# Moving running sums, shifts and part of a modulation from GpSimd to VectorE, in a kernel whose instruction order is planned

## The chip, the cores and the metric

The kernel runs on one core of a Trainium2 chip. The metric is the device time of one launch in microseconds (us), as a median over runs. A core has TensorE (matrix products), VectorE, ScalarE and GpSimd (elementwise work), and SyncE, which issues the transfers. In the profile they are PE (its weight loads: PEld), DVE, ACT, POOL and SP. Each engine takes its own instructions in the order in which they are written and waits for others by semaphores.

## The reference

One step of a decoder of two layers, in float32. A layer is an FFN, a token mixing and a second FFN, each with a modulation before it and a LayerNorm after it:

```
h = x * (1 + sc1) + sh1
x = layer_norm(ALPHA * x + 0.5 * (1 + gt1) * swiglu(h, wi1, wo1))
h = x * (1 + sc2) + sh2
x = layer_norm(ALPHA * x + (1 + gt2) * mixing(h))
h = x * (1 + sc3) + sh3
x = layer_norm(ALPHA * x + 0.5 * (1 + gt3) * swiglu(h, wi2, wo2))
```

Shift, scale and gate come from conditioning vectors by a matrix of 1024 x 9216 per layer (the "ada" matrix). There are 256 tokens of one new sequence (the prompt), which share one conditioning vector, and 4 new tokens of each of 8 older ones (the samples), with a vector each. The mixing has four recurrent mixers side by side (retention, GLA, HGRN2, gated delta rule), worked in chunks; the last needs the inverse of a triangular matrix per chunk. Outputs are the activations and the updated states.

## The kernel before

Activations lie with the 1024 channels on partitions, as 8 tiles (index k or m) of 128 x 288: 256 prompt columns and 32 sample columns. For float32 accuracy each operand of a big matmul is split in a rounded part and a rest: ScalarE writes the rounded weights (`whi`), VectorE the rest (`wlo`, a subtraction over 512 columns), and a product takes three matmuls of 288 columns (`mm3`). Activations are split likewise into `hh` and `hl`. Weights stream in by transfers of 512 KB into rings of staging buffers (`st`, `stg`).

The parts that matter here:

- `modulate` (L780) makes h = x * A + B for one tile: ScalarE the prompt columns, where A and B are one number per channel; the sample columns take a multiplication and an addition of 128 x 32, on VectorE for tile 0 and on GpSimd for tiles 1 to 7. Then ScalarE rounds and VectorE subtracts. It is called in each norm that has a successor (five of them) and at the start of the program.
- `residual` (L820) adds the gated product to x for tile m, lets ScalarE square it, and GpSimd adds tile and square to a running sum `ss` of 128 x 576: for m = 1 to 6 in an FFN, for m = 1 to 4 after the mixing (`FSUM`, `WSUM`). The tiles after that go to the LayerNorm's statistics by matmuls of their own (`norm_stats`).
- `shift` (L809) subtracts the mean of the first residual tile from the others, for the accuracy of the variance. In an FFN these are 7 subtractions of 128 x 288 on GpSimd. After the mixing (`wout`, with `SUBENG` 2) they are 8, of which 5 are on GpSimd. `wout` has two parts: six of the eight mixer tiles first, the shift, then the last two tiles and the residuals.
- Other work on GpSimd stays where it is: clearing, small copies, the causal mask of the delta rule, sums of the rotary embedding, and the products of the state update (`vx`, `S0`). In the last norm four subtractions of the mean are on GpSimd.

The order of all instructions is planned on the host. The program records operations with their dependences (`Rec.add`), gives each a priority (the longest path of costs to the end, plus boosts), and `schedule` (L305) then places them one after another: it takes the engine that is free first and its ready operation of highest priority. What this fixes is the order on each engine; the chip keeps to it and takes its own time. `LB` holds boosts by the part of the program (`inv0` is the inverse of layer 0, `gates0` the eight gate projections, `glf0` the projections of GLA), for all engines or for one. `PEN` is how much priority ScalarE gives up to keep its loaded function table, `PACE` spaces filler work such as the ada matrix.

Of the kernel before, what the change touches and what calls it, by code (L numbers as in the profile page):

```python
# [19 lines left out]
DMA_LAT = 2.0  # L20
LOOK, STAY = 40, 20
SWITCH = 0.19
PEN, PACE = 5, 2
HOLD, HFRAC = {'DVE': 20, 'ACT': 20}, 0.6
LB = {'hg1': 12, 'retf0': -29, 'gdnf1': 15, 'wout1': -4, 'gla1': -3, 'hgf1': 16, 'gdnb1': 19, 'norm11': -4, 'norm01': -8, ('ret1', 'DVE'): 10, 'norm00': -20, ('norm02', 'DVE'): -20, ('ffn12', 'DVE'): -23, 'glf1': -8, 'hgf0': -15, 'ffn11': -26, ('inv0', 'ACT'): -15, 'norm02': -15, ('norm12', 'DVE'): 2, ('norm11', 'ACT'): 2, ('ret0', 'DVE'): 15, 'ffn12': 22, ('norm00', 'DVE'): 8, 'norm12': 62, ('glf0', 'PE'): 8, ('inv1', 'PE'): 8, 'ffn01': 7, 'gdnb0': -4, ('retf1', 'ACT'): 12, ('ffn02', 'DVE'): -2, ('norm00', 'PE'): 8, 'retf1': -8, ('gdnf1', 'DVE'): 4, ('ffn01', 'ACT'): -15, ('wout1', 'DVE'): -30, 'hg0': -30, ('gates1', 'DVE'): 6, ('gdnf1', 'PE'): -15, ('inv0', 'DVE'): -4, 'norm10': -53, ('gdnb0', 'DVE'): 30, 'inv0': 4, ('norm10', 'PE'): 2, 'wout0': -4, ('hgf0', 'ACT'): -30}
WIN, WARM, WARMUP = 3.413, 0.3, 20.0
KEEP, KEEP2 = 0, 0.05
DMA_RATE = 350e3
# [93 lines left out]


class Op:
    __slots__ = ("i", "eng", "fn", "args", "kw", "cost", "succ", "nd", "rt", "touch", "prio", "aset", "end", "nbytes", "start", "like", "label", "why", "prev", "act", "tiled", "boost", "side")


class Eng:
# [9 lines left out]
class Rec:  # L138
# [59 lines left out]
    def add(self, eng, attr, fn, args, kw):  # L198
        if fn == "activation" and isinstance(kw.get("bias"), (float, int)) and kw["bias"] == 0:
            kw.pop("bias")  # L200
        o = Op()
        o.i = len(self.ops)
        o.eng, o.fn, o.args, o.kw = eng, (attr, fn), args, kw
        out = args[0]
        ins = [v for v in list(args[1:]) + list(kw.values()) if isinstance(v, LV)]
        outs = [out] if isinstance(out, LV) else []
        o.cost = self.cost(eng, fn, out, ins, kw, args)
        o.act, o.tiled, o.side = 0.0, (128, 128), None
        if eng == "PE" and fn == "matmul":
            n = prod(args[2].shape[1:])  # L210
            side = lambda n: 32 if n <= 32 else 64 if n <= 64 else 128
            o.tiled = (side(args[1].p1 - args[1].p0), side(out.p1 - out.p0))
            if args[1].dtype != F32R and o.tiled != (128, 128):
                o.side = kw.get("tile_position") or (0, 0), 2 * ((out.p1 - out.p0) / 1200 + 0.006), 4 * n / 2400 + 0.003
            area = (args[1].p1 - args[1].p0) * (out.p1 - out.p0) / 16384
            o.act = area * (n / 2400 if args[1].dtype == F32R else n / 600)
        o.nbytes = 0
        if fn == "dma_start":
            v = out if isinstance(out, LV) else args[1]
            o.nbytes = 4 * prod(v.shape)  # L220
            if eng == "POOL":
                o.cost = 0.15
        rw = fn == "copy_predicated" or (fn == "matmul" and kw.get("start") is False)
        o.aset = ACT_SET.get(args[2]) if fn == "activation" else None
        deps, touch = set(), {}
        for v in ins + (outs if rw else []):
            r = v.region()
            touch[id(v.t)] = v.t
            for (j, w, q) in v.t.acc:
                if w and j != o.i and overlap(q, r):  # L230
                    deps.add(j)
            v.t.acc.append((o.i, False, r))
        for v in outs:
            r = v.region()
            touch[id(v.t)] = v.t
            keep = []
            for (j, w, q) in v.t.acc:
                if j != o.i and overlap(q, r):
                    deps.add(j)
                    if covers(r, q):  # L240
                        continue
                elif j == o.i and covers(r, q):
                    continue
                keep.append((j, w, q))
            keep.append((o.i, True, r))
            v.t.acc[:] = keep
        if fn == "matmul":

            start, single = kw.get("start", True), kw.get("start", True) and kw.get("stop", True)
            q0, q1 = out.p0 // 32, (out.p1 + 31) // 32  # L250
            for (j, a, b, one) in out.t.mms:
                if j != o.i and a < q1 and q0 < b and (not (single and one) if start else one is not None):
                    deps.add(j)
            out.t.mms.append((o.i, q0, q1, single if start else None))
        o.touch = list(touch.values())
        for t in o.touch:
            t.left += 1
        o.succ, o.nd, o.rt, o.prio, o.like, o.label, o.why = [], 0, 0.0, 0.0, self.fill, self.label, ('start', -1)
        o.nd, o.boost = len(deps), self.boost + LB.get(self.label, 0.0) + LB.get((self.label, eng), 0.0)
        for j in deps:  # L260
            self.ops[j].succ.append(o.i)
        self.ops.append(o)
        return o
# [41 lines left out]
    def schedule(self):  # L305
# [15 lines left out]
        busy = dict.fromkeys(engs, 0.0)  # L321
        dense, run, tiled = False, 0, (128, 128)
        tiles = {}
        win, wact, warm = 0, 0.0, False
        recent, racts = collections.deque(), 0.0

# [32 lines left out]
        while len(order) < len(ops):  # L359
            best = None  # L360
            for e in engs:
                if avail[e]:
                    t = free[e]
# [64 lines left out]
            if e == "PE":  # L428
                a = o.act
                if o.tiled != tiled:  # L430
                    tiled, run = o.tiled, 0
                    c += SWITCH
                    tiles = {}
                f = 1 if warm else 2
                if o.side:

                    (r0, c0), ld, st = o.side
                    w = max([x for (r1, c1), x in tiles.items() if (r1 == r0 or tiled[0] == 128) and (c1 == c0 or tiled[1] == 128)], default=0.0)
                    extra = max(0.0, w - t)
                    late = t + (c - o.cost) + extra + f * max(ld, st)  # L440
                    tiles[r0, c0] = late
                    c += extra - o.cost + ld
                run += 1
                recent.append((t, a))
                racts += a
                if not warm:
                    c += 0.0 if o.side else o.cost
                b = (win + 1) * WIN
                if t + c > b:
                    wact += a * (b - t) / c  # L450
                    n = int((t + c) / WIN)
                    warm = wact / WIN > WARM or n > win + 1 and a > WARM * c
                    win, wact = n, a * (t + c - n * WIN) / c
                else:
                    wact += a
            if o.aset is not None and o.aset != cur:
                cur = o.aset
                c += 1.28
# [164 lines left out]
class Net:  # L623
# [156 lines left out]
    def modulate(self, k, xs, A, B, hh, hl, h=None, cuts=((0, NT),)):  # L780

        nc = self.nc
        if h is None:
            h = self.tmp()
        for c0, c1 in cuts:
            c1 = min(c1, TP)
            if MODACT:
                nc.scalar.activation(h[:, c0:c1], xs[:, c0:c1], AF.Identity, bias=B[:, k, 0:1], scale=A[:, k, 0:1])
            else:
                nc.vector.tensor_scalar(h[:, c0:c1], xs[:, c0:c1], A[:, k, 0:1], B[:, k, 0:1], op0=ALU.mult, op1=ALU.add)  # L790
        hs = h[:, TP:].rearrange("p (b t) -> p b t", t=TS)
        eng = nc.gpsimd if k else nc.vector
        eng.tensor_tensor(hs, xs[:, TP:].rearrange("p (b t) -> p b t", t=TS), bc(A[:, k, 1:9], 2, TS), op=ALU.mult)
        eng.tensor_tensor(hs, hs, bc(B[:, k, 1:9], 2, TS), op=ALU.add)
        for c0, c1 in cuts:
            o = nc.scalar.activation(hh[:, k, c0:c1], h[:, c0:c1], AF.Copy)
        nc.vector.tensor_sub(hl[:, k, :], h, hh[:, k, :])
        return o
# [10 lines left out]
    def shift(self, x0, first, tag, nv=0):  # L809
# [4 lines left out]
        self.mm(psc, self.ones128, x0)  # L814
        nc.scalar.activation(c, psc, AF.Copy)
        for j in range(first, KD):
            (nc.vector if j <= nv else nc.gpsimd).tensor_tensor(xa[:, j, :], xa[:, j, :], c, op=ALU.subtract)
        return c

    def residual(self, m, ps, G, nsum, slast=1, shifted=False):  # L820
# [18 lines left out]

            nc.scalar.activation(self.t([P, 1], "pre"), d[:, m, 1, 0:1], AF.Exp, scale=-1.0)  # L840
        if m == 1:
            nc.gpsimd.tensor_tensor(ss, d[:, 0, :, :], d[:, 1, :, :], op=ALU.add)
        elif 1 < m < nsum:
            nc.gpsimd.tensor_tensor(ss, ss, d[:, m, :, :], op=ALU.add)
        nc.boost = 0.0
        self.nsum, self.slast = nsum, slast

# [1242 lines left out]
```

## Time and profile before

| | |
|---|---|
| runs | 1537.78 us median of 3 (1537.45 to 1544.69) |
| profiled execution | 1532.65 us, span on the core 1530.8 us |
| mean granted TensorE clock | 0.967 of full speed |
| busy | TensorE 1446.6, VectorE 909.5, ScalarE 712.5, GpSimd 226.0 us |
| HBM | 263.52 MB read, 176 GB/s over the span |

The busy time of an engine counts instructions from start to end; back to back they overlap by a little, as the next begins before the last one has left the pipeline. A matmul of 288 columns is shown with about 0.3 us, while one starts every 0.133 us at full clock. Nearly all lines are L539, the one that emits each planned operation, so groups are told apart by their tiles. "Chain" is the work that ended last, followed back from the end: at each step to what released it.

### The profile page before, as it was taken

What the parts mean: (1) busy time and instruction counts of PE and PEld (TensorE: products, weight loads), DVE (VectorE), ACT (ScalarE), POOL (GpSimd) and SP (SyncE); (2) the same over time, 40 slices, a digit from 0 to 9 for tenths busy, and PEclk for the clock granted to TensorE, in tenths of its full rate; (3) what the DMA queues carried; (4) which work ended last, traced back from release to release, by engine and by line L of the source; (5) the groups of instructions that cost most, each with busy time, mean ns of one, the idle gap of its engine ahead of it and who ended that gap; (6) DMA issues with size and microseconds to landing.
All of it is one profiled execution on the core that took longest, in us unless ns stands there. A gap on an engine that the chain in (4) does not pass through costs nothing.

```text
span 1530.8 us, 32584 instructions
## 1 busy us (share of the span) xinstructions
PE 1446.6 (94%) x13172; PEld 1353.6 (88%) x13172; DVE 909.5 (59%) x1922; ACT 712.5 (47%) x1449; POOL 226.0 (15%) x347
## 2 busy tenths in 40 slices
PE   7899998989998989999999999988999997999996
PEld 6899998888986869999999999977888885999996
DVE  3555555867366895555565555477269578555564
ACT  4544434853312465444474444476132644644443
POOL 0000023210013340002120003132000325000031
PEclk9999999999999999999999999998599999999998
DMA  9856576655445655555555556455032364555530
GB/s 359 327 179 209 177 264 202 232 184 180 159 171 189 214 207 181 166 165 168 168 213 183 165 166 208 150 176 184 27 97 65 112 218 176 194 166 165 166 123 31
DMA packets 80215, 271.11 MB, mean 177 GB/s; under 512 B 9376, under 2 KB 12992, under 8 KB 80064
## 3 DMA queue, kind: packets, MB, share of 16 engines
q1 hardware_dynamic: 80064, 269.03, 52.6%
q8 instruction: 103, 1.69, 0.4%
q14 instruction: 48, 0.39, 0.1%
HBM read 263.52 MB, written 5.47 MB: 176 GB/s over the span
## 4 chain that ended last, share of the span: by engine, by line
PE 81%; DVE 9%; ACT 5%; issue 2%; DMA 2%; SPq 0%; POOL 0%; DVEq 0%; ACTq 0%; POOLq 0%
PE psum_acc L539 48%; PE psum_ps L539 25%; PE psum_ada L539 3%; DVE base_d L539 3%; PE psum_phB L539 2%; PE psum_phA L539 2%; DVE base_wlo L539 1%; ACT base_whi L539 1%; ACT base_tmp L539 1%; ACT L538 1%; PE psum_oa L539 1%; DVE base_tmp L539 1%; DMA gp_stg<-wi 1%; DMA base_st<-win 1%; DVE mx_qxA L539 1%
## 5 line engine op out<-in xcount | busy, mean ns | idle before, releaser
L539 ACT ACTIVATE base_whi<-base_st 128x512 fp32r<-128x512 f32 x410 | 252.1, 624 | 271.1 <-PE psum_acc L539 205.2
L539 DVE TENSOR_TENSOR base_wlo<-base_st,base_whi 128x512 fp32r<-128x512 f32 x410 | 294.1, 725 | 135.4 <-ACT base_whi L539 123.8
L539 DVE TENSOR_TENSOR gp_wlog<-gp_stg,gp_whig 128x512 fp32r<-128x512 f32 x274 | 198.1, 727 | 279.6 <-ACT gp_whig L539 278.5
L539 ACT ACTIVATE gp_whig<-gp_stg 128x512 fp32r<-128x512 f32 x274 | 171.4, 628 | 297.7 <-PE psum_acc L539 261.5
L539 PE MATMUL psum_ps<-base_hh,base_whi 128*128 128x288 f32 x760 | 192.0, 299 | 4.1 <-ACT base_hh L539 4.1
L539 PE MATMUL psum_ps<-base_hl,base_whi 128*128 128x288 f32 x760 | 186.2, 297 | 0.8 <-DVE base_hl L539 0.8
L539 PE MATMUL psum_ps<-base_hh,base_wlo 128*128 128x288 f32 x760 | 185.7, 296 | 0.0
L539 PE MATMUL psum_acc<-base_hh,gp_whig 128*128 128x288 f32 x648 | 168.1, 304 | 8.0 <-ACT base_hh L539 5.0
L539 PE MATMUL psum_acc<-base_hh,base_whi 128*128 128x288 f32 x552 | 162.0, 326 | 13.9 <-ACT base_hh L539 7.1
L539 PE MATMUL psum_acc<-base_hl,gp_whig 128*128 128x288 f32 x648 | 162.5, 296 | 0.0
L539 PE MATMUL psum_acc<-base_hh,gp_wlog 128*128 128x288 f32 x648 | 157.2, 296 | 0.0
L539 PE MATMUL psum_acc<-base_hl,base_whi 128*128 128x288 f32 x552 | 155.8, 312 | 0.4
L539 PE MATMUL psum_acc<-base_hh,base_wlo 128*128 128x288 f32 x552 | 155.0, 312 | 0.4 <-DVE base_wlo L539 0.4
L539 PEld LDWEIGHTS psum_ps<-base_hh,base_whi 128*128 128x128 f32 x760 | 132.5, 190 | 6.2 <-ACT base_hh L539 4.6
L539 PEld LDWEIGHTS psum_ps<-base_hl,base_whi 128*128 128x128 f32 x760 | 130.2, 189 | 1.7 <-DVE base_hl L539 1.5
L539 PEld LDWEIGHTS psum_ps<-base_hh,base_wlo 128*128 128x128 f32 x760 | 130.2, 189 | 0.2
L539 PEld LDWEIGHTS psum_acc<-base_hh,base_whi 128*128 128x128 f32 x552 | 104.5, 200 | 26.2 <-ACT base_hh L539 7.8
L539 PEld LDWEIGHTS psum_acc<-base_hh,gp_whig 128*128 128x128 f32 x648 | 112.6, 189 | 13.0 <-ACT base_hh L539 6.9
L539 PE MATMUL psum_acc<-gp_gl,gp_whig 128*128 128x288 f32 x384 | 113.9, 297 | 0.0
L539 PE MATMUL psum_acc<-gp_gh,gp_whig 128*128 128x288 f32 x384 | 113.8, 296 | 0.0
L539 PE MATMUL psum_acc<-gp_gh,gp_wlog 128*128 128x288 f32 x384 | 113.2, 295 | 0.0
L539 PEld LDWEIGHTS psum_acc<-base_hl,gp_whig 128*128 128x128 f32 x648 | 112.4, 189 | 0.3 <-DVE base_hl L539 0.2
(429 smaller groups left out, 2773.4 us busy)
## 6 DMA issues: line engine op xcount, KB each, us to landing
base_ast<-ada_w SPq DMA_DIRECT2D x135, 512.0 KB, 6.5
gp_stg<-wi SPq DMA_DIRECT2D x82, 512.0 KB, 3.6
base_st<-wi SPq DMA_DIRECT2D x82, 512.0 KB, 3.6
base_st<-win SPq DMA_DIRECT2D x60, 512.0 KB, 3.6
gp_stg<-wo SPq DMA_DIRECT2D x48, 512.0 KB, 3.5
base_st<-wo SPq DMA_DIRECT2D x40, 512.0 KB, 3.5
base_st<-wout SPq DMA_DIRECT2D x16, 512.0 KB, 4.6
gp_stg<-wi SPq DMA_DIRECT2D x14, 256.0 KB, 6.8
```

What stands on the lines that cost most here:

```text
L538: nc.scalar.preload_act_table_set(cur)
L539: getattr(getattr(nc, o.fn[0]), o.fn[1])(*[conv(a) for a in o.args], **{k: conv(v) for k, v in o.kw.items()})
```

## The change

Sums, shifts and the samples' modulation are issued on VectorE for all tiles. The planner gets a rule: an operation `tensor_tensor` or `tensor_sub` on VectorE or GpSimd without an operand in PSUM is marked `port`; if the other engine has such a one running at the time it is placed, its cost grows by what is left of that. Two constants and 32 boosts change.

```diff
-PEN, PACE = 5, 2
+PEN, PACE = 8, 1.5
...
-LB = {
...
-'gla1': -3, 'hgf1': 16, 'wout0': -4, 'inv0': 4, ('inv0', 'ACT'): -15, ('glf0', 'PE'): 8, 'norm10': -53, 'norm12': 62
+'gla1': 5, 'hgf1': 8, 'wout0': 15, 'inv0': -11, ('inv0', 'ACT'): -45, 'glf0': 30, 'norm10': -31, 'norm12': 88
+('glf0', 'ACT'): 30, 'gates0': -8, ('gates0', 'DVE'): 2, 'gates1': 4, 'ret1': 4
...
+        o.port = eng in ("DVE", "POOL") and fn in ("tensor_tensor", "tensor_sub") and not any(v.t.tag.pool == "psum" for v in ins)
...
+        port = {"DVE": (0.0, 0.0), "POOL": (0.0, 0.0)}
...
+            if o.port:
+                a, b = port["POOL" if e == "DVE" else "DVE"]
+                if a <= t < b:
+                    c += b - t
+                port[e] = t, t + c
...
-        eng = nc.gpsimd if k else nc.vector
-        eng.tensor_tensor(hs, xs[:, TP:].rearrange("p (b t) -> p b t", t=TS), bc(A[:, k, 1:9], 2, TS), op=ALU.mult)
-        eng.tensor_tensor(hs, hs, bc(B[:, k, 1:9], 2, TS), op=ALU.add)
+        nc.vector.tensor_tensor(hs, xs[:, TP:].rearrange("p (b t) -> p b t", t=TS), bc(A[:, k, 1:9], 2, TS), op=ALU.mult)
+        nc.vector.tensor_tensor(hs, hs, bc(B[:, k, 1:9], 2, TS), op=ALU.add)
...
-            (nc.vector if j <= nv else nc.gpsimd).tensor_tensor(xa[:, j, :], xa[:, j, :], c, op=ALU.subtract)
+            nc.vector.tensor_tensor(xa[:, j, :], xa[:, j, :], c, op=ALU.subtract)
...
-            nc.gpsimd.tensor_tensor(ss, d[:, 0, :, :], d[:, 1, :, :], op=ALU.add)
+            nc.vector.tensor_tensor(ss, d[:, 0, :, :], d[:, 1, :, :], op=ALU.add)
...
-            nc.gpsimd.tensor_tensor(ss, ss, d[:, m, :, :], op=ALU.add)
+            nc.vector.tensor_tensor(ss, ss, d[:, m, :, :], op=ALU.add)
```

The boost of `inv1` (8 on TensorE) stays.

## Rows read from the trace of the kernel before

**Rows 1.** The page: busy us of each engine, share of the span, instructions.
```profile
PE 1446.6 (94%) x13172; PEld 1353.6 (88%) x13172; DVE 909.5 (59%) x1922; ACT 712.5 (47%) x1449; POOL 226.0 (15%) x347
```

**Rows 2.** The page's chain of waits: share of the span by engine.
```profile
PE 81%; DVE 9%; ACT 5%; issue 2%; DMA 2%; SPq 0%; POOL 0%; DVEq 0%; ACTq 0%; POOLq 0%
```

**Rows 3.** Table of stretches: busy us per engine, granted clock, DMA share, GB/s.
```profile
core 0: us, PE busy (x) PEld busy (x) DVE busy (x) ACT busy (x) POOL busy (x), PEclk, DMA share, GB/s
380.00:450.00 70.00, 68.96 (x1125) 63.50 (x1123) 34.50 (x68) 16.17 (x36) 3.19 (x4) 1.00 0.47 156
518.00:556.00 38.00, 36.10 (x330) 29.55 (x328) 31.43 (x78) 15.95 (x35) 12.44 (x12) 1.00 0.38 126
716.00:776.00 60.00, 60.00 (x452) 60.00 (x451) 33.94 (x57) 27.85 (x47) 16.08 (x13) 1.00 0.51 156
...
1060.00:1120.00 60.00, 57.64 (x740) 52.43 (x740) 23.56 (x53) 18.50 (x39) 0.61 (x1) 0.72 0.19 63
1262.00:1290.00 28.00, 23.20 (x193) 15.44 (x192) 23.79 (x53) 10.39 (x26) 17.22 (x18) 0.94 0.28 96
```

**Rows 4.** VectorE's timeline, layer 0's output projection: start, duration, operation.
```profile
544.48 0.18 DVE L539 TENSOR_TENSOR base_d<-base_rt,base_xa 128x32 f32<-128x32 f32 x1
544.58 0.87 DVE L539 SCALAR_TENSOR_TENSOR base_d<-psum_ps,base_G,base_xa 128x256 f32<-128x256 f32 x2
545.37 1.93 DVE L539 TENSOR_TENSOR base_wlo<-base_st,base_whi 128x512 fp32r<-128x512 f32 x1
...
552.61 0.94 DVE L539 TENSOR_TENSOR base_d<-base_rt,base_xa 128x32 f32<-128x32 f32 x1
```

**Rows 5.** GpSimd's timeline in the same stretch.
```profile
545.34 1.41 POOL L539 TENSOR_TENSOR base_d<-base_d 128x576 f32<-128x576 f32 x1 [3.61 <-issue]
```

**Rows 6.** The chain in order of time: start, length, what.
```profile
309.65 2.38 DVE base_tmp L539
...
1225.55 1.37 DVE base_wlo L539
...
1278.54 1.40 DVE base_d L539
...
1283.36 1.90 DVE base_wlo L539
```

**Rows 7.** GpSimd's groups: count, busy us, mean ns, idle before and its releaser.
```profile
L539 POOL TENSOR_TENSOR base_d<-base_d 128x576 f32<-128x576 f32 x32 | 45.6, 1425 | 162.5 <-ACT base_d L539 158.8 <-issue 3.6
L539 POOL TENSOR_TENSOR base_xa<-base_xa,base_tmp 128x288 f32<-128x288 f32 x38 | 37.9, 1023 | 475.9 <-ACT base_tmp L539 457.2 <-DVE base_xa L539 14.8 <-issue 3.7
...
L539 POOL TENSOR_TENSOR base_d<-base_d,base_hA 128x32 f32<-128x32 f32 x35 | 12.9, 368 | 39.2 <-DVE base_d L539 31.9 <-DVE base_tmp L539 7.2
...
L539 POOL TENSOR_TENSOR base_tmp<-base_tmp,base_hB 128x32 f32<-128x32 f32 x7 | 2.1, 314 | 0.1
```

**Rows 8.** VectorE's timeline where GpSimd is idle: pairs of equal instructions.
```profile
562.14 0.81 DVE L539 TENSOR_TENSOR base_d<-base_d 128x288 f32<-128x288 f32 x2
...
577.55 1.29 DVE L539 TENSOR_TENSOR base_wlo<-base_st,base_whi 128x512 fp32r<-128x512 f32 x2
```

**Rows 9.** VectorE's timeline in layer 0's first norm.
```profile
269.54 0.49 DVE L539 TENSOR_TENSOR base_d<-base_d 128x288 f32<-128x288 f32 x1
...
270.69 0.50 DVE L539 TENSOR_TENSOR base_d<-base_d 128x288 f32<-128x288 f32 x1
```

**Rows 10.** Timelines of VectorE and GpSimd in the conv of layer 0.
```profile
298.87 0.54 DVE L539 SCALAR_TENSOR_TENSOR base_tmp<-base_tmp,base_cvec,base_tmp 128x312 f32<-128x312 f32 x1
...
298.87 0.60 POOL L539 COPY mx_gcso<-base_tmp 128x3 f32<-128x3 f32 x2 [0.82 <-ACT base_tmp L539]
```

**Rows 11.** ScalarE's groups: the loads of function tables.
```profile
L538 ACT ACT_TABLE_LOAD x30 | 38.5, 1283 | 1.2 <-PEq L2077 0.7
```

**Rows 12.** The chain in the two inverses.
```profile
401.58 1.99 PE psum_ps L539 x64
...
1083.60 3.56 PE psum_ps L539 x64
1087.16 1.02 PE psum_acc L539 x3
```

More of the change, by code (lines that the diff above doesn't have):

```diff
@@ L22 @@
 SWITCH = 0.19
-PEN, PACE = 5, 2
+PEN, PACE = 8, 1.5
 HOLD, HFRAC = {'DVE': 20, 'ACT': 20}, 0.6
-LB = {'hg1': 12, 'retf0': -29, 'gdnf1': 15, 'wout1': -4, 'gla1': -3, 'hgf1': 16, 'gdnb1': 19, 'norm11': -4, 'norm01': -8, ('ret1', 'DVE'): 10, 'norm00': -20, ('norm02', 'DVE'): -20, ('ffn12', 'DVE'): -23, 'glf1': -8, 'hgf0': -15, 'ffn11': -26, ('inv0', 'ACT'): -15, 'norm02': -15, ('norm12', 'DVE'): 2, ('norm11', 'ACT'): 2, ('ret0', 'DVE'): 15, 'ffn12': 22, ('norm00', 'DVE'): 8, 'norm12': 62, ('glf0', 'PE'): 8, ('inv1', 'PE'): 8, 'ffn01': 7, 'gdnb0': -4, ('retf1', 'ACT'): 12, ('ffn02', 'DVE'): -2, ('norm00', 'PE'): 8, 'retf1': -8, ('gdnf1', 'DVE'): 4, ('ffn01', 'ACT'): -15, ('wout1', 'DVE'): -30, 'hg0': -30, ('gates1', 'DVE'): 6, ('gdnf1', 'PE'): -15, ('inv0', 'DVE'): -4, 'norm10': -53, ('gdnb0', 'DVE'): 30, 'inv0': 4, ('norm10', 'PE'): 2, 'wout0': -4, ('hgf0', 'ACT'): -30}
+LB = {'hg1': 12, 'retf0': -29, 'gdnf1': 15, 'glf0': 30, 'wout1': -6, 'gla1': 5, 'hgf1': 8, 'gdnb1': 19, 'norm11': -2, ('ret1', 'DVE'): 10, 'norm00': -20, ('norm02', 'DVE'): -20, ('ffn12', 'DVE'): -23, 'ret1': 4, 'glf1': -10, 'hgf0': -15, 'ffn11': -26, ('inv0', 'ACT'): -45, 'norm02': -15, ('norm12', 'DVE'): 2, ('norm11', 'ACT'): 2, ('ret0', 'DVE'): 15, 'ffn12': 22, ('norm00', 'DVE'): 6, 'norm12': 88, ('inv1', 'PE'): 8, 'ffn01': 7, 'gdnb0': -6, ('retf1', 'ACT'): 12, ('ffn02', 'DVE'): -2, ('norm00', 'PE'): 12, 'retf1': -8, ('gdnf1', 'DVE'): 4, ('ffn01', 'ACT'): -15, ('wout1', 'DVE'): -30, 'hg0': -30, ('gates1', 'DVE'): 6, ('gdnf1', 'PE'): -15, ('inv0', 'DVE'): -4, 'norm10': -31, ('gdnb0', 'DVE'): 30, 'inv0': -11, ('norm10', 'PE'): 2, 'wout0': 15, ('hgf0', 'ACT'): -30, ('gla0', 'PE'): 2, ('hgf1', 'PE'): -4, 'gdnf0': -2, ('gates1', 'ACT'): -15, ('norm12', 'ACT'): 30, ('gla1', 'ACT'): -15, ('retf0', 'ACT'): 8, 'gates0': -8, ('glf0', 'ACT'): 30, ('norm02', 'ACT'): -4, ('norm00', 'ACT'): -4, ('gates0', 'DVE'): 2, ('wout1', 'ACT'): -30, ('gdnf1', 'ACT'): -2, 'gates1': 4}
 WIN, WARM, WARMUP = 3.413, 0.3, 20.0
@@ L124 @@
 class Op:
-    __slots__ = ("i", "eng", "fn", "args", "kw", "cost", "succ", "nd", "rt", "touch", "prio", "aset", "end", "nbytes", "start", "like", "label", "why", "prev", "act", "tiled", "boost", "side")
+    __slots__ = ("i", "eng", "fn", "args", "kw", "cost", "succ", "nd", "rt", "touch", "prio", "aset", "end", "nbytes", "start", "like", "label", "why", "prev", "act", "tiled", "boost", "side", "port")
 class Eng:
```

## The prediction, made before the change was run

> **What bounds the kernel now.** I read the engine shares first: TensorE is busy for 94% of the span, VectorE 59%, GpSimd 15% [rows 1]. The chain of waits puts 81% of the span on TensorE, 9% on VectorE, 5% on ScalarE and 0% on GpSimd [rows 2]. These averages hide two kinds of stage, so I read a table of stretches next [rows 3]. In the second matmul of an FFN (716 to 776 us) TensorE is busy 60.00 of 60 us, VectorE 33.94, GpSimd 16.08: whatever VectorE or GpSimd do there is covered. Around the mixers' output projection (518 to 556 and 1262 to 1290 us) VectorE is busy 31.43 of 38 and 23.79 of 28 us, and in the second TensorE only 23.20 of 28: there VectorE sets the pace. The triangular inverse of layer 0 lies in 380 to 450 us at a granted clock of 1.00 (2.4 GHz); that of layer 1 in 1060 to 1120 us at a mean of 0.72, so more than half of that stretch is at 1.2 GHz.
>
> Last I read VectorE instruction by instruction beside GpSimd. In layer 0's output projection an addition of two 32-column tiles takes 0.18 us at 544.48, but 0.94 at 552.61, and a 512-column subtraction takes 1.93 us at 545.37 [rows 4]. The long subtraction lies beside a GpSimd running sum, 1.41 us from 545.34 [rows 5], and its excess is about as long as that sum. There are four such instructions in that stretch. Layer 1 has them on the chain itself: 1.40 us at 1278.54 for a 32-column addition, 1.90 us at 1283.36 for a 512-column subtraction [rows 6]. So two elementwise instructions on SBUF tiles, one on each engine, run in turn.
>
> **The change part by part.**
>
> *What leaves GpSimd.* 32 running sums (45.6 us), 38 shift subtractions (37.9 us) and 42 pairs of modulation, which are four groups from 12.9 to 2.1 us, 29.6 together [rows 7]: 113 of its 226 us. What comes to VectorE is counted from one start to the next. 32-column instructions are 0.18 us long and start 0.10 apart (544.48 and 544.58 [rows 4]), so ends overlap by 0.08. Two of 512 columns end to end take 1.29 us and two of 288 take 0.81 [rows 8]: alone 0.69 and 0.45, apart 0.60 and 0.37. By that slope 576 columns cost 0.67 (an estimate). Sum: 32 x 0.67 + 38 x 0.37 + 84 x 0.10 = 44 us more VectorE work, less the time for which it was held by the work that moves.
>
> *In the FFNs* (6 sums and 7 shifts each): 6 x 0.67 + 7 x 0.37 = 6.6 us, beside a TensorE that is full while VectorE has 26 of 60 us free [rows 3]. Cost 0. Queued behind a sum are the splits of later weights; these run ahead of their matmuls by several tiles, so they can slip by a sum. If the last one can't, 0.67 us per FFN: 2.7 us, kept for the range.
>
> *In the two output projections* (4 sums and 5 shifts each). VectorE gets 4 x 0.67 + 5 x 0.37 = 4.5 us more. In layer 0 it loses what the sums held it: four instructions, the first by 1.93 - 0.69, the last by 0.94 - 0.18, together 3.8 us. So VectorE taken alone ends up 0.7 us later: one end. The other end takes both engines as one resource, as they run in turn: a sum shrinks from 1.42 to 0.67 us, a shift from 1.02 (the mean [rows 7]) to 0.37; 4 x 0.75 + 5 x 0.65 = 6.3 us earlier. Layer 1's stretch is nearer the second end (GpSimd busy 17.22 of 28 us), layer 0's nearer the first (12.44 of 38) [rows 3]. I take the middle, 2.5 us in each: -5. The state updates queued on GpSimd behind the shifts come earlier; nothing on the chain waits for them.
>
> *In the norms* (7 pairs each). Before the mixers VectorE works without a pause through three 288-column operations per tile, 1.15 us from 269.54 to 270.69 [rows 9]. A pair adds 0.20 us if other work lies between its halves, 0.39 if not (two of 0.18, and a gap). It removes some 0.05 us of hold (0.49 and 0.50 there, 0.45 undisturbed). So 7 x 0.15 = 1 us each in the two norms before mixers: +2. Before an FFN the twelve matmuls of a tile (12 x 0.133, from 452 in 60 us) take 1.6 us, longer than VectorE's turn, and the first tile was on VectorE already: 0. At the start of the program the pairs lie behind transfers: 0. Ends: +13.7 (5 norms x 7 x 0.39) and -2 (5 x 7 x 0.05, where only the hold goes).
>
> *The planner's new rule.* 17 instructions on the chain are held by work that stays on GpSimd (state updates, the causal mask, rotary sums), together 12.6 us over their undisturbed lengths. The first is the product of 2.38 us at 309.65 (288 columns, 0.45 undisturbed), the last the subtraction of 1.37 us at 1225.55 [rows 6]. The planner now sees such a wait when it places what follows, but it places by priority and looks for no way round it. Ends 0 and -12.6; I take a third: -4.
>
> In the conv a three-operand instruction on SBUF tiles takes 0.54 us beside two GpSimd copies, which take 0.60 [rows 10]; held for them it would end no earlier than 1.1 us after its start. The Trainium skill (SBUF — State Buffer, section "SBUF: two separate sides") says that any VectorE instruction with two SBUF inputs and any GpSimd instruction that reads SBUF shut each other out. The trace agrees for the additions above and does not for this copy. By the page the planner's rule, which knows two-operand arithmetic only, would misplace the 36 conv instructions, and less of the 4 us would be won; by the row it misses nothing there.
>
> *PEN 5 to 8.* ScalarE loads a table 30 times, 38.5 us [rows 11], 1.28 each. A higher penalty may save loads; one saved on the chain gives 1.28. Ends 0 and -13 (ten of them); I take two: -2.5.
>
> *PACE and the boosts* reorder everything within a stage. The trace shows what an order can be worth: a group of 64 small inverse matmuls takes 1.99 us in layer 0 and 3.56 in layer 1, and the big ones between layer 1's groups 1.02 for three, 0.34 each [rows 12] against 0.133. Layer 1 has four groups of 64 and four of 32 in this state, and some 24 big ones: 4 x 1.57 + 4 x 0.79 + 24 x 0.2 = 14 us. So layer 1 could win up to 14 us and layer 0 lose as much. I take 0, and keep both ends.
>
> Sum: -5 + 0 + 2 - 4 - 2.5 + 0 = -9.5 us. The profiled execution took 1532.65 us (1530.8 of span and 1.85 around it), 5.1 less than the median of the timed runs, 1537.78; so it would go to 1523.2 and the median to 1528.3. I say **1528 us**, with its own range from 1519 to 1535.
>
> **The rivals.** Half a per cent, 7.7 us, is about what a measurement of this kernel can tell from no change.
> - *A better order too* (1514 us). The new priorities also put projections among layer 1's inverse, its clock stays at 2.4 GHz, and the 14 us come on top. For it: that stretch moves 63 GB/s only [rows 3], so weights could be brought there. Against it: inv1's own boosts stay as they are.
> - *Layer 0's inverse loses its cover* (1549 us, slower). The diff puts inv0 from 4 to -11, its ScalarE work from -15 to -45, and glf0 up to 30, so the projections that now lie between its groups can be spent before it. Then layer 0 pays the 14 us; the output projections and norms still give 3, planner and tables nothing: 1537.8 - 3 + 14. It decides from a mean granted clock under about 0.8 in that stretch. Against it: gates0, eight projections, goes down to -8 and is left to fill.
> - *Nothing comes of it* (1539 us). VectorE takes on as much as it was held (0.7 us late at one output projection, even at the other), the norms cost 2 and a saved load pays for it; the planner places as before. For it: GpSimd is 0% of the chain [rows 2].
>
> **How the numbers follow.** Forecast 0.45, better order 0.15, lost cover 0.2, nothing 0.2. Faster by over 0.5% (under 1530.1): 0.15 and four fifths of 0.45, so 0.51. Slower by over 0.5% (above 1545.5): 0.2 and some of the dear end of the norms, 0.22. Between them 0.27. The range takes in most of the first rival and the second up to its price: 1511 to 1549.
>
> **What would show it.** GpSimd busy near 113 us, VectorE between 915 and 935. In the residuals no 32-column addition over 0.3 us. The second part of each output projection up to the norm some 2.5 us shorter. Tiles before the mixers every 1.3 us instead of 1.15. Fewer than 30 table loads. The clock over both inverses, which tells the first two rivals apart. The prediction is wrong if the sums push weight splits so far that TensorE waits in the FFNs, or if the order moves a whole stage by more than 10 us.

## The result, and the profile after

The kernel after takes 1526.4 us (median of 6 runs, 1518.8 to 1533.59); the kernel before, run beside it, 1543.64 (6 runs, 1537.45 to 1545.15). The ratio is 0.9898, with an interval of 0.9863 to 0.9933. Later, on another chip, it was 1522.38 and 0.9879 (0.9850 to 0.9907). So it is faster by 1.0 to 1.2%, and 1528 was near. It was near for the wrong reasons, as the experiments show.

The engine shares of the kernel after answer to [rows 1], its chain to [rows 2]:

```profile
PE 1450.7 (95%) x13172; PEld 1355.8 (89%) x13172; DVE 922.0 (60%) x2076; ACT 710.4 (47%) x1447; POOL 112.9 (7%) x193
```
```profile
PE 81%; DVE 9%; DMA 4%; ACT 4%; issue 1%; SPq 0%; ACTq 0%; DVEq 0%; POOL 0%
```

GpSimd lost exactly the 113 us that were moved, VectorE has 922, and the chain is as it was. Nothing here tells where the 17 us came from, so I cut the span into stages: each ends with the last matmul of a LayerNorm's statistics. They are FFN, mixing of layer 0, FFN; FFN, mixing of layer 1, FFN; the rest is the last norm. The profile of before that I had was an unusually quick execution (1532.65 us at a clock of 0.967; 62 timed runs with a clock on record have a median of 1542.6 at 0.959), so a second profile of before stands here (1540.51 us, 0.959), then the kernel after (1528.0 us). The columns are those of [rows 3]:

```profile
core 0: us, PE busy (x) PEld busy (x) DVE busy (x) ACT busy (x) POOL busy (x), PEclk, DMA share, GB/s
0.00:261.22 261.22, 246.47 (x2313) 236.95 (x2313) 130.72 (x272) 116.82 (x227) 28.88 (x49) 0.99 0.71 243
261.22:564.91 303.69, 281.25 (x3119) 243.24 (x3123) 202.16 (x461) 127.07 (x271) 61.97 (x97) 0.91 0.53 182
564.91:787.50 222.59, 218.47 (x1625) 215.81 (x1629) 127.65 (x245) 114.54 (x228) 24.59 (x34) 0.98 0.57 179
787.50:1011.60 224.10, 222.11 (x1855) 219.54 (x1858) 123.02 (x240) 109.50 (x219) 25.09 (x36) 1.00 0.55 179
1011.60:1297.89 286.29, 264.87 (x2570) 226.72 (x2573) 195.87 (x448) 129.73 (x274) 61.47 (x101) 0.92 0.38 126
1297.89:1526.15 228.26, 221.68 (x1708) 218.30 (x1708) 121.57 (x236) 109.19 (x220) 21.12 (x28) 0.99 0.47 152
```
```profile
0.00:254.41 254.41, 242.16 (x2252) 232.91 (x2256) 132.98 (x295) 119.00 (x229) 5.62 (x17) 1.00 0.71 249
254.41:563.84 309.43, 289.62 (x3194) 249.16 (x3194) 199.78 (x488) 125.07 (x270) 49.57 (x79) 0.90 0.53 182
563.84:785.29 221.45, 216.78 (x1603) 215.08 (x1607) 131.67 (x271) 115.25 (x228) 3.63 (x7) 0.98 0.54 176
785.29:1010.32 225.03, 222.68 (x1862) 219.57 (x1866) 126.11 (x267) 109.56 (x219) 3.99 (x10) 1.00 0.56 180
1010.32:1292.11 281.79, 263.12 (x2674) 224.89 (x2674) 197.24 (x472) 127.91 (x275) 46.61 (x77) 0.95 0.42 143
1292.11:1513.88 221.77, 216.39 (x1600) 214.19 (x1599) 125.40 (x262) 108.33 (x218) 0.25 (x1) 0.99 0.44 138
```

The differences are -6.8, +5.7, -1.1, +0.9, -4.5 and -6.5, with -0.2 in the last norm -12.5 us. So these profiles have the gain in the first and the last FFN, and the two mixings nearly cancel. Look at TensorE's instruction counts: the first FFN has 61 matmuls fewer, the last 108 fewer, and the mixings have them: by their tiles 60 and 104 of these are small matmuls of the ada matrix, which the planner uses as filler. Look then at the clock in the mixings: lower in layer 0, higher in layer 1. The stretches of [rows 3] show it closer up, in the kernel after:

```profile
380.00:450.00 70.00, 66.36 (x865) 60.71 (x864) 28.90 (x63) 13.21 (x29) 0.61 (x1) 0.74 0.47 163
1060.00:1120.00 60.00, 57.29 (x560) 53.36 (x558) 40.53 (x91) 29.69 (x60) 4.27 (x14) 0.96 0.42 135
```

In the first profile of before these were 1.00 and 0.72, in the second 0.83 and 0.71. The chain says it by groups of 64 small matmuls of the inverse, as in [rows 12] (start, length, what); the first row is layer 0's, the second layer 1's:

```profile
423.56 3.56 PE psum_ps L547 x64
...
1147.25 1.99 PE psum_ps L547 x64
```

Four of layer 0's five groups of 64 now take what four of layer 1's took, and layer 1's take what layer 0's took. But part of this was there before: in one order, the same group of layer 0 ran at either rate (first profile of before, then the second):

```profile
416.59 1.99 PE psum_ps L539 x64
...
415.91 3.56 PE psum_ps L539 x64
```

The clock did what the two rivals on the order said, one in each layer. The price did not follow: against the second profile layer 0's mixing pays 5.7 us and layer 1's gets 4.5, of 14 each. Against the first, from which the prediction was made, it is 16.0 and 7.1. In TensorE's order layer 1's inverse has 369 matmuls of 288 columns between its first and last group, 50 before. Layer 0's has as many as before (285 for 288), but none between its last eight groups, where 96 stood.

### The profile page after: what moved, and what is told of

It reads as the page before. It is cut to its first block, busy times and chain, and to the rows that moved or that the text cites. A ratio compares the mean times of both kernels' runs of the same rounds, so it can differ in the third digit from the quotient of the medians.

```text
span 1526.2 us, 32521 instructions
## 1 busy us (share of the span) xinstructions
PE 1450.7 (95%) x13172; PEld 1355.8 (89%) x13172; DVE 922.0 (60%) x2076; ACT 710.4 (47%) x1447; POOL 112.9 (7%) x193
## 4 chain that ended last, share of the span: by engine, by line
PE 81%; DVE 9%; DMA 4%; ACT 4%; issue 1%; SPq 0%; ACTq 0%; DVEq 0%; POOL 0%
PE psum_acc L547 47%; PE psum_ps L547 24%; DVE base_d L547 3%; PE psum_ada L547 3%; PE psum_phA L547 3%; PE psum_phB L547 3%; DMA base_st<-win 2%; PE psum_oa L547 1%; ACT base_tmp L547 1%; DMA base_ast<-ada_w 1%; DVE base_wlo L547 1%; ACT base_whi L547 1%; DVE base_hl L547 1%; DVE base_tmp L547 1%; DVE base_xa L547 1%
## 5 line engine op out<-in xcount | busy, mean ns | idle before, releaser
L547 DVE TENSOR_TENSOR base_wlo<-base_st,base_whi 128x512 fp32r<-128x512 f32 x410 | 282.9, 698 | 143.4 <-ACT base_whi L547 133.2
L547 DVE TENSOR_TENSOR gp_wlog<-gp_stg,gp_whig 128x512 fp32r<-128x512 f32 x274 | 188.0, 690 | 262.3 <-ACT gp_whig L547 241.9
L547 PE MATMUL psum_ps<-base_hh,base_whi 128*128 128x288 f32 x760 | 197.6, 301 | 8.2 <-ACT base_hh L547 7.9
L547 PE MATMUL psum_ps<-base_hl,base_whi 128*128 128x288 f32 x760 | 191.1, 298 | 0.0
L547 PE MATMUL psum_ps<-base_hh,base_wlo 128*128 128x288 f32 x760 | 189.8, 298 | 0.5 <-DVE base_wlo L547 0.5
L547 PEld LDWEIGHTS psum_ps<-base_hl,base_whi 128*128 128x128 f32 x760 | 133.3, 191 | 0.5 <-DVE base_hl L547 0.4
```

The costliest lines, as they stand in the source:

```text
L547: getattr(getattr(nc, o.fn[0]), o.fn[1])(*[conv(a) for a in o.args], **{k: conv(v) for k, v in o.kw.items()})
```

## The experiments

First the direct work. The planner was left as in the kernel before, and so was the order; in the traces TensorE's and ScalarE's instructions stand in the same order one for one, and only the engine that executes the moved operations changes (`Eng` takes the engine to plan for and the one to issue on):

```diff
+        self.moved = Eng(self, "POOL", "vector")
...
-        eng = nc.gpsimd if k else nc.vector
+        eng = nc.moved if k else nc.vector
...
-            nc.gpsimd.tensor_tensor(ss, ss, d[:, m, :, :], op=ALU.add)
+            nc.moved.tensor_tensor(ss, ss, d[:, m, :, :], op=ALU.add)
```

> The kernel before with its planned order kept to the last instruction: the sums, shifts and samples' modulation are planned as GpSimd work with GpSimd's costs, and only issued on VectorE. It measures the move by itself. My theory (the move gives a little, the order the rest): 2 to 6 us faster than before, GpSimd busy 113 us, no 32-column addition in a residual over 0.3 us. 'All of it is the order': within 2 us of before. 'All of it is the end of the mutual holds': 12 to 18 us faster, as the changed kernel.

Measured 1546.0 us, ratio 1.0009 (0.9998 to 1.0019): the move by itself gains nothing. The holds did go. VectorE in layer 0's output projection, to be held against [rows 4]; the third row is a running sum:

```profile
553.22 0.18 DVE L540 TENSOR_TENSOR base_d<-base_rt,base_xa 128x32 f32<-128x32 f32 x1
553.32 0.87 DVE L540 SCALAR_TENSOR_TENSOR base_d<-psum_ps,base_G,base_xa 128x256 f32<-128x256 f32 x2
554.11 0.75 DVE L540 TENSOR_TENSOR base_d<-base_d 128x576 f32<-128x576 f32 x1
554.77 0.69 DVE L540 TENSOR_TENSOR base_wlo<-base_st,base_whi 128x512 fp32r<-128x512 f32 x1
...
560.36 0.18 DVE L540 TENSOR_TENSOR base_d<-base_rt,base_xa 128x32 f32<-128x32 f32 x1
```

Of 48 such 32-column additions none takes over 0.2 us; before, nine took over 0.3, the longest 1.40. But a sum costs VectorE 0.66 us from start to start. From the first residual addition to the end of the stage it is 10.73 us in layer 0 (second profile of before: 11.89) and 13.91 in layer 1 (14.47): 1.2 and 0.6 us gained (the shifts lie before this stretch). The norms before mixers lose what was forecast: a tile takes 1.30 us instead of the 1.15 of [rows 9] (the two halves of a tile's pair now stand among its three operations),

```profile
268.63 0.45 DVE L540 TENSOR_TENSOR base_hl<-base_d,base_hh 128x288 fp32r<-128x288 f32 x1
...
269.94 0.45 DVE L540 TENSOR_TENSOR base_hl<-base_d,base_hh 128x288 fp32r<-128x288 f32 x1
```

and the last tile's split comes 0.6 and 1.4 us later after the norm's statistics. The two middle FFNs are 0.8 and 0.9 us longer (223.35 and 224.98), the first is the same; the last is 1.4 us shorter, with 3.4 us less at 1.2 GHz.

The counterpart is the kernel after, planned as it is, with the moved operations executed on GpSimd again:

```diff
+        self.moved = Eng(self, "DVE", "gpsimd")
...
-        nc.vector.tensor_tensor(hs, hs, bc(B[:, k, 1:9], 2, TS), op=ALU.add)
+        eng = nc.moved if k else nc.vector
+        eng.tensor_tensor(hs, hs, bc(B[:, k, 1:9], 2, TS), op=ALU.add)
```

> The changed kernel with its planned order kept, and the moved work issued on GpSimd again. It undoes the move by itself. My theory: 8 to 14 us faster than before, so 3 to 8 us slower than the changed kernel. 'All of it is the order': 13 to 18 us faster than before, like the changed kernel. 'All of it is the end of the holds': within 3 us of before.

Measured 1527.38 us, ratio 0.9882 (0.9855 to 0.9909): the whole gain is there without the move. (The profiled execution, 1515.54 us at a clock of 0.977, was the quickest of the six.) GpSimd's groups show its work back, and eight of the 32-column additions take over 0.3 us again, up to 1.32:

```profile
L548 POOL TENSOR_TENSOR base_d<-base_d 128x576 f32<-128x576 f32 x32 | 47.4, 1482 | 159.8 <-ACT base_d L548 146.4 <-issue 13.0
L548 POOL TENSOR_TENSOR base_xa<-base_xa,base_tmp 128x288 f32<-128x288 f32 x38 | 36.3, 987 | 151.9 <-ACT base_tmp L548 150.7 <-DVE base_xa L548 1.2
```

The stretch from the first residual addition to the end of the stage, which the prediction wanted 2.5 us shorter, is 10.1 and 10.7 us in the kernel after (1.8 and 3.8 less than before), and 9.8 and 10.0 here, without the move. So it is the order. Which part of the change makes it? The kernel after with all constants of before, boosts included, and the kernel after without the rule:

```diff
-PEN, PACE = 8, 1.5
+PEN, PACE = 5, 2
...
-LB = {
+LB = {
...
```

> The changed kernel with PEN, PACE and all boosts of before: the move and the planner's rule, without the new constants. My theory (the constants carry most of the order's gain): between 8 us faster and 10 us slower than before, and slower than the changed kernel by 8 us or more. 'The rule and the move do it, the constants are detail': 12 to 18 us faster than before.

Measured 1542.65 us, ratio 0.9993 (0.9980 to 1.0006), inside my range. Its profile has 704 ada matmuls in the first FFN, as before, and 64 of the 104 in the last; these two take 262.7 and 227.3 us.

```diff
-            if o.port:
+            if False:
```

> The changed kernel with the planner's rule off (no operation pays for the other engine): the move and the new constants. If the rule is what matters in the planning: 5 us or more slower than the changed kernel, and more than 5 us of held VectorE time on the chain again. If the move and the constants do it: within 4 us of the changed kernel. I expect 3 to 10 us slower than the changed kernel.

Measured 1541.74 us, ratio 0.9990 (0.9972 to 1.0009): 15 us slower than the changed kernel, more than I expected. In its profile layer 0's mixing takes 318.9 us, with 75.1 us at 1.2 GHz, and the last FFN 227.6, with 64 ada matmuls; the kernel after has 309.4, 64.9, 221.8 and none. I read the two results as "only all three together give the good order". The next kernel, the one before with the new constants and nothing else, refuted that:

```diff
-PEN, PACE = 5, 2
+PEN, PACE = 8, 1.5
...
-LB = {
...
+'gla1': 5, 'hgf1': 8, 'wout0': 15, 'inv0': -11, ('inv0', 'ACT'): -45, 'glf0': 30, 'norm10': -31, 'norm12': 88
...
```

> The kernel before with the new PEN, PACE and LB alone: nothing is moved to VectorE and the planner doesn't know the rule. Its planned order has two features of the kernel after that the kernel before lacks: some 500 matmuls of gates and norms stand between the groups of layer 1's inverse (before: 136), and some 50 of the modulation's matmul pairs have left the last feed-forward. Theory A (the gain is those features of the order, wherever they come from): 1524 to 1533 us, the profile shows layer 1's inverse at about 29 ns per matmul and the last feed-forward near 222 us. Theory B (the constants were fitted to one planner and give a good order only with the rule and the move): 1540 to 1547 us, as the two kernels with half of the change measured. Theory C (the move is needed at run time after all, because the new order brings GpSimd's work against VectorE's): the order's features are there but the stretches with running sums, shifts and modulation are longer, 1535 to 1540 us.

Measured 1515.32 us (1502.73 to 1520.51), ratio 0.9819 (0.9786 to 0.9852): theory A, and more than it expected. This beats the kernel after, with GpSimd as busy as ever (227.2 us). Its first, layer 1's and last stage:

```profile
0.00:255.63 255.63, 243.06 (x2252) 233.95 (x2256) 129.41 (x268) 118.81 (x229) 26.39 (x44) 1.00 0.71 247
...
1006.75:1278.17 271.42, 254.25 (x2655) 216.21 (x2658) 194.59 (x448) 127.48 (x272) 63.11 (x100) 0.97 0.44 144
1278.17:1500.51 222.34, 217.60 (x1623) 214.63 (x1623) 121.76 (x236) 109.02 (x221) 21.64 (x28) 0.99 0.46 143
```

The first and the last stage are nearly as in the kernel after, and layer 1's mixing is 10 us shorter still, at a clock of 0.97. Does the move help in this better order? The same order with the moved operations issued on VectorE (the edit of the first experiment, with the new constants):

```diff
+        self.moved = Eng(self, "POOL", "vector")
...
-PEN, PACE = 5, 2
+PEN, PACE = 8, 1.5
```

> The kernel before with the new PEN, PACE and LB, and the running sums, shift and samples' modulation issued on VectorE; they are planned as GpSimd's, so that the order is exactly that of the kernel with the constants alone (1515.3 us), which leaves them on GpSimd. Theory A (what GpSimd holds on VectorE costs nothing in any of these orders): 1512 to 1519 us, the same. Theory B (the move is worth its 5 us where the order doesn't waste it): 1507 to 1511 us. Theory C (VectorE's extra work is late in the mixings, where it is busiest): 1519 to 1526 us.

Measured 1516.78 us, ratio 0.9852 (0.9811 to 0.9893). This overlaps the one above, so no gain is seen again; a loss of some us can't be told from none, as six runs of this order spread over 13 us.

Another order for layer 1's mixing, found by changing nine boosts of the kernel after:

```diff
+('glf1', 'ACT'): 2, ('gla0', 'ACT'): -11, ('ret1', 'PE'): -15, ('norm11', 'ACT'): -6, 'gdnb1': 15, 'hg1': 16
...
```

> The kernel after with nine boosts changed, eight of them labels of the mixings; first feed-forward, layer 0's mixing and the two middle feed-forwards are planned as in the kernel after, layer 1's mixing gets another order. Theory A (the order decides, and each covered stretch of TensorE is worth its microseconds): stages up to layer 1's mixing within 1 us of the kernel after at the same granted clock, layer 1's mixing 3 to 8 us shorter, 1518 to 1524 us. Theory B (orders of this quality differ by chance, about 15 us between any two): anywhere from 1520 to 1545 us, and the earlier stages move too. Theory C (the granted clock evens it out): 1526 us, the gained time comes back as stretches at half clock.

Measured 1524.83 us, ratio 0.9897 (0.9871 to 0.9923). The earlier stages repeat within 0.5 us and layer 1's mixing is 5.2 us shorter in the profile (276.6), both as theory A said. The median, though, is that of the kernel after (1522.38 beside it) and just outside theory A's range; theory C can't be told from A by this.

Second profiles of both kernels:

> The kernel after unchanged, a second profile. Theory A (times of one order follow where TensorE falls to half clock): 1518 to 1534 us; the four feed-forward stages repeat within 0.5 us, the two mixings differ between the two executions by 0.2 to 0.5 us for each us more at half clock. Theory B (the scatter comes from the DMAs): the feed-forwards differ too, by a us or more, at the same half-clock time.

> The kernel before unchanged, a second profile, since the first was of an execution of 1532.65 us, under all its timed runs. Theory A (its scatter is the half clock in layer 0's mixing): 1539 to 1548 us, layer 0's mixing near 302 us with over 40 us at half clock, all other stages within 1.5 us of the first profile. Theory B (the first profile's execution was quick in all stages): every stage 0.5 to 2 us longer.

Before: 1540.51 us, mixing of layer 0 303.7 us instead of 293.4, with 54.6 us at 1.2 GHz instead of 27.3 in the same order; other stages within 2.6 us, where theory A allowed 1.5. After: 1522.38 us in the median, the profiled execution 1531.37; its other FFNs and both mixings repeat within 0.2 us, but the first FFN is 2.9 us longer (with 3.4 us at 1.2 GHz for none), which theory A didn't allow. One order is thus not one time: some stretches fall to half clock in one execution and not in the next.

Last, the two features of the new order (matmuls among layer 1's inverse, ada matmuls out of the last FFN) one at a time in the kernel before, each by one number, and `PACE`:

```diff
+'inv1': -4
```

> The kernel before with one number changed: layer 1's inverse has a boost of -4. Everything up to layer 1's mixing is planned as before; there, 429 matmuls of gates and projections stand between the groups of the inverse, before 136; ten of the modulation's pairs more than before leave the last feed-forward. Theory A (layer 1's inverse at half clock is what the mixing loses): its groups go from 53 to about 29 ns per matmul, layer 1's mixing is 6 to 11 us shorter, 1532 to 1537 us. Theory B (the cover costs what it gives, since the matmuls between the groups delay the inverse and the projections wait for it): 1540 to 1545 us though the clock is up. Theory C (the half clock moves elsewhere): 1540 to 1545 us, with the same microseconds at half clock in another place.

Measured 1535.96 us, ratio 0.9975 (0.9951 to 0.9999), in theory A's range for the time. In its profile the inverse's first groups still run at half clock before the later ones take 1.99 us per 64; but the mixing takes 285.98 us, as before, which is what theory B says of it. The median clock of its runs is 0.9645 against 0.959. Where its gain lies is thus not shown.

```diff
+('inv1', 'DVE'): 8
```

> The kernel before with one number changed: VectorE's work of layer 1's inverse has a boost of 8. Everything up to layer 1's mixing is planned as before and the inverse has the same 137 matmuls between its groups; 62 of the modulation's pairs (124 matmuls) have gone from the last feed-forward into layer 1's mixing. Theory A (they fill gaps in the mixing, while the feed-forward has none): the last feed-forward goes from 227 to 222 us, the mixing is 0 to 2 us longer, 1538 to 1541 us. Theory B (TensorE's work is only moved): the mixing is 4 to 5 us longer, 1542 to 1545 us.

Measured 1545.01 us, ratio 1.0026 (1.0001 to 1.0052): theory B, and worse. Layer 1's mixing and the last FFN:

```profile
1011.66:1310.79 299.13, 278.22 (x2676) 237.38 (x2675) 196.46 (x449) 129.42 (x274) 62.49 (x101) 0.90 0.38 126
1310.79:1533.76 222.97, 217.01 (x1600) 214.01 (x1598) 121.51 (x234) 109.16 (x221) 22.87 (x28) 0.99 0.47 149
```

The FFN gains 5.3 us, as expected; the mixing pays 12.8, as its clock falls to 0.90.

```diff
-PEN, PACE = 5, 2
+PEN, PACE = 5, 1.5
```

> The kernel before with PACE 1.5 for 2. The plan has 60 of the modulation's matmuls fewer in the first feed-forward and nearly none in the last; layer 0's inverse has 202 matmuls between its groups for 465 before, layer 1's 137 for 136. Theory A (modulation out of the full stages gains, an inverse without cover loses): first stage 255 to 256 us (before 261), last feed-forward 222 us (before 227), layer 0's mixing 308 to 315 us with over 55 us at half clock, layer 1's as before: 1540 to 1546 us. Theory B (each constant gives a good order by itself): 1528 to 1536 us. Theory C (a planner off its fitted constants is bad all over): over 1550 us.

Measured 1559.79 us, ratio 1.0136 (1.0095 to 1.0176). First stage, layer 0's mixing, last stage:

```profile
0.00:255.12 255.12, 242.94 (x2252) 233.36 (x2256) 129.28 (x268) 118.69 (x229) 26.61 (x44) 1.00 0.72 248
255.12:579.12 324.00, 296.06 (x3175) 250.57 (x3178) 203.18 (x464) 123.84 (x270) 62.63 (x102) 0.88 0.50 170
...
1321.27:1544.19 222.92, 217.01 (x1599) 214.12 (x1598) 121.53 (x234) 109.16 (x221) 22.88 (x28) 0.99 0.47 149
```

The FFNs and layer 0's mixing have the signs of theory A, but the mixing pays 20 us, more than it allowed, and layer 1's is 7.6 us longer (293.9), where it said as before. The time is in theory C's range, though two of the six stages are better than before.

## What sets the time of a mixing

The profiles of all these kernels give 14 executions of each mixing. For each I took its length, its ada matmuls and the microseconds at 1.2 GHz by the trace's record of the clock:

| kernel | layer 0: us, ada, at 1.2 GHz | layer 1: us, ada, at 1.2 GHz |
|---|---|---|
| before, first and second profile | 293.4, 886, 27.3; 303.7, 886, 54.6 | 288.9, 340, 51.2; 286.3, 340, 44.4 |
| after, first and second profile | 309.4, 956, 64.9; 309.5, 956, 61.4 | 281.8, 444, 30.7; 282.0, 444, 30.7 |
| before's order, moved | 302.0, 886, 44.4 | 290.3, 340, 58.0 |
| after's order, GpSimd | 304.1, 956, 41.0 | 273.3, 444, 10.2 |
| old constants | 301.9, 960, 44.4 | 285.3, 380, 34.1 |
| no rule | 318.9, 956, 75.1 | 280.5, 380, 23.9 |
| constants alone | 304.3, 948, 51.2 | 271.4, 424, 13.7 |
| constants alone, moved | 302.1, 948, 51.2 | 277.5, 424, 23.9 |
| nine boosts changed | 309.5, 956, 54.6 | 276.6, 422, 27.3 |
| cover alone | 303.2, 886, 54.6 | 286.0, 346, 37.5 |
| ada alone | 303.7, 886, 51.2 | 299.1, 444, 61.4 |
| PACE alone | 324.0, 936, 78.5 | 293.9, 444, 47.8 |

A least-squares line through all 14 is 252 + 0.029 x ada + 0.51 x (us at 1.2 GHz) for layer 0 and 255 + 0.028 x ada + 0.50 x (us at 1.2 GHz) for layer 1; it leaves 2.4 and 2.2 us. The clock's factor is known to 0.06 and 0.05 (one standard error). The first factor is hardly known: its error is 0.024 and 0.016. It does not disagree with a row of the second profile of before, which has 64 such matmuls on the chain in 1.88 us, 29 ns each:

```profile
446.62 1.88 PE psum_ada L539 x64
```

The clock's factor can be held against half the rate. The Trainium skill (TensorE: Matmul & The Clock Gate, section "Terms") puts the penalty at the throttled time times one minus the clock's share, so 0.5 us per us; the line agrees with 0.51 and 0.50. The order held still gives less: the two executions of the kernel before differ by 10.3 us for 27.3 us at 1.2 GHz in layer 0's mixing and by 2.6 for 6.8 in layer 1's, 0.38 us per us.

By the line the kernel after pays, against the second profile of before, 2.0 us for 70 more ada matmuls in layer 0's mixing and 5.2 us for its clock (5.7 measured); in layer 1's 2.9 us for 104 more, and gets 6.9 back for its clock (-4.5 measured). In the last FFN, where TensorE is busy for 97%, the filler costs more: 104 matmuls fewer give 5.3 us in the experiment with ada alone, against the second profile of before. That profile has 6.8 us at 1.2 GHz in this FFN and the experiment 3.4; the first profile, with 3.4 too, takes 227.0 us, so 4.0 are the filler's, 39 ns each. The first stage gets 6.1 us from `PACE` alone; TensorE is busy 3.5 us less there and idle 2.6 us less. With 60 matmuls fewer that is 100 ns each, more than they take, so other things change with them; which is not shown. An estimate from these prices: moving all 164 out of the two FFNs gives 4.0 + 6.1, costs 164 x 0.029 = 4.8 in the mixings, and leaves 5 us, if the clock stays as it was.

The runs have a clock without a profile. In 62 runs of the kernel before, a clock higher by 0.01 goes with 10.6 us less (correlation -0.81); 0.01 of a span of 1540 us is 30.8 us at 1.2 GHz, so this is 0.34 us per us, near the 0.38 above. At equal clock the kernel after's 12 runs are 10.4 us under that line; the rest of its 17 and 20 us is its higher clock (medians 0.964 and 0.9675 against 0.959). The clock is not the whole of an order: on the same line the constants alone lie 15.5 us under it, and the old constants, no rule and `PACE` alone 7.9, 6.8 and 10.7 us above. The two kernels that share the kernel after's order part here too: with the work back on GpSimd the six runs lie 5.2 us under the line, and reach the same time by a higher clock (0.9685). Whether the held VectorE work raises the clock is not shown.

## Why the prediction was right, and where it was wrong

The time was met, the sum behind it was not. The sum took 9.5 us off 1537.78, the median of three runs; with three more, the kernel before has 1543.64, and the fall was 17.2 us. A start 5.9 us too low and a fall 7.7 us too small nearly cancel.

- *The output projections, -5.* This step failed: "I take the middle, 2.5 us in each". Measured with the order held still: -1.2 and -0.6. The nearer end was VectorE taken alone: what it was held, it now spends on the sums. The sign that the prediction named, this stretch 2.5 us shorter, did come (1.8 and 3.8), but from the order: without the move it is shorter still.
- *The norms, +2.* Right: +0.6 and +1.4, at the 1.30 us per tile that was named.
- *The FFNs, 0.* Wrong by 0.8 and 0.9 us in the middle two; the order of the constants alone repeats it, with 1.1 and 1.0 between its two forms, the kernel after's order does not (-0.1 and +0.6). Where it shows, the price kept for the range (0.67 each) was the one to take. With these terms the move in the kernel before's order is worth -1.7 + 2.0 + 1.7 = +2.0 us; the median rose by 2.4. That these agree is in part chance, as layer 1's mixing is 4.0 us longer at 13.6 us more half clock.
- *The rule, -4.* Failed as a price: it was read from time held on the chain, and that time does not set the kernel's. Summed over VectorE's two-operand instructions on the chain, the time beyond their undisturbed length beside GpSimd is about 21 us before and 5 after. The move alone leaves 14, the move and the rule with the old constants 0.5; their medians are 1546.0 and 1542.65. The fastest kernel has no rule and 13 us held. What the rule is worth by itself can't be told from the order that it redraws: adding it to the move with the old constants gives 3.4 us, removing it from the kernel after costs 15, and adding it and the move to the constants alone costs 7 to 11.
- *Tables, -2.5.* Two loads fewer, as forecast (28 for the 30 of [rows 11]); all four orders planned with `PEN` 8 have 28. But the move and the rule with `PEN` 5 have 26, so the number is not the work of `PEN` alone. What the loads gave was not measured.

```profile
L546 ACT ACT_TABLE_LOAD x28 | 35.9, 1283 | 1.2 <-PEq L2084 0.7
```

- *The order, 0 with ends of 14.* This is the term that was the result, and it failed in what it left out. It looked at the two inverses alone, and there 0 was near: the two mixings together are +1.2 us against the second profile of before. Filler leaving the FFNs was in no term, since *In the FFNs* asked only whether VectorE has room; yet the first and the last FFN are 6.8 and 6.5 us shorter, more than the whole difference of the spans, 12.5. (An estimate by 0.38 to 0.5 us per us: about 3 of these 13.3 are the clock's, which is at 1.2 GHz for 6.8 us less in the two.)

The sign of being wrong, a whole stage moved by more than 10 us, is met against the first profile of before (layer 0's mixing, +16.0) and not against the second (+5.7). The direct terms, -9.5 forecast, are not seen in any time that was measured with the order held still; the order gave the -17, and with the constants alone -27. That 1528 was near is chance.

Open remain: why the same order falls to half clock in one execution and not in the next; which of the 32 boosts make the constants good; and why the first FFN gains more than its filler takes.

## What to carry to other kernels

Where an order is planned, an edit of costs, engines or constants draws a new order: hold the order still and move the work, or hold the work and change the order, before saying what either is worth. Here nine orders spread over 1515 to 1560 us, while moving 113 us of GpSimd's work to VectorE changed the median by 1 to 2.4, no change clear of the noise. Time held on the chain is not time won: 0.5 us held went with 1542.65 and 13 with 1515.32. And price a stage by TensorE's clock and by where its filler stands before looking at waits of other engines.

## What the hardware showed that I had not expected

- Relieving VectorE of holds of up to 1.4 us gained nothing measurable in three orders (+2.4, -1.0 to the kernel after's first median, and +1.5 us).
- A stretch with groups of small matmuls may run at either clock level in the same order: the same 64 matmuls of layer 0's inverse took 1.99 and 3.56 us in two executions of the kernel before, and its mixing has 27.3 and 54.6 us at 1.2 GHz, 10 us apart in length.
- The same small matmul takes 29 ns in a row of 64 on the chain, and the last FFN is 39 ns longer for each of 104 of them.
- The planner's rule is right to leave out what reads PSUM: in the kernel before 57 two-operand instructions of VectorE with an operand there ran beside GpSimd's two-operand arithmetic, none over 0.02 us above its usual length. But a three-operand one on SBUF tiles can be held, which the rule does not mark: 0.89 us for 0.30 at 1521.18 in the last norm, beside a GpSimd subtraction of 128 x 288.
